# Sums over heads by moving the squares, products in two column halves, inverses from 16-row blocks

## The chip, the cores and the metric

One core of a Trainium2 chip runs the whole program. Its engines are PE (TensorE, matrix products; its weight loads have a row of their own, PEld), DVE (VectorE), ACT (ScalarE), POOL (GpSimd) and SP, which here only issues DMAs. The metric is the device time of one execution in microseconds (us); of three runs of the kernel before, the median was 831.88 us (831.33 to 832.63).

## The reference

Two decoder layers in float32 on 512 tokens of width 1024. Layer 0 mixes tokens with an RWKV-7 recurrence over 16 heads of 64 channels; layer 1 is a causal differential attention over shared keys and values. Each layer ends with a gated embedding ("ple"): `p[i] @ ple_w[i]`, gated by `sigmoid(h @ ple_gate[i])`. What the change touches:

```python
kk = k * k_k.reshape(H, N)
kk = kk / jnp.maximum(jnp.linalg.norm(kk, axis=-1, keepdims=True), 1e-12)
...
def step(state, inp):
    r_t, w_t, k_t, v_t, kk_t, a_t = inp
    s_kk = jnp.einsum('bhij,bhj->bhi', state, kk_t)
    state = (state * w_t[:, :, None, :]
             - s_kk[..., None] * (kk_t * a_t)[:, :, None, :]
             + v_t[..., None] * k_t[:, :, None, :])
    return state, jnp.einsum('bhij,bhj->bhi', state, r_t)
...
y = y + jnp.sum(r * k * r_k, axis=-1, keepdims=True) * v
...
e = p[i] @ ple_w[i]
g = jax.nn.sigmoid(h @ ple_gate[i])
h = h + rms_norm(g * e, ple_norm[i])
```

There are two sums over the 64 channels of a head for every token: the squared norm of `kk`, and the bonus `r * k * r_k`.

## The kernel before

**Dense products.** Every dense product is split in three fp32r products (`mm3`, L280 to L282: high by high, high by low, low by high), each 128x128 weights against 512 columns. There are 800 such triples. For each weight half-matrix of 512 columns (a "half") 32 triples run: 8 channel tiles by 4 blocks. The order of the halves in layer 0 is the table ORDER (L36): r, k and v of the first half of the channels, then of the second, then the two halves of the gate g. The ple products (16 triples a layer) come behind them (ple(0), L1331) and, for layer 1, behind its last projection.

**Recurrence.** The 16 heads are 8 channel tiles of two heads; tiles 0 to 3 are group 0 and 4 to 7 group 1. The 512 tokens are 8 chunks of 64. For each group: `decay(i)` (L668) makes the decays of a tile; `k_evac(i)` (L742) makes the scaled keys and both sums over heads; `gram` (L846) makes the 128x128 products of keys and queries of one pair of chunks, masked on DVE (L873); `inverse(n)` (L886, four batches) inverts the 64x64 unit triangular matrices of 16 heads-and-chunks; `operands` (L997) transposes and loads; `recur` (L1028) walks over the chunks; `finish` (L1132) normalises and gates.

**Sums over heads before.** `k_evac` holds the squares as weights (128x128 of `sq`) and moves the selector `hsel`, 2 columns wide: four products per tile (L756) for the norm, four (L789) with `rksel` for the bonus. An fp32 product is two records in the trace, so 32 instructions of a line are x64 there.

**Inverse before.** The 32x32 diagonal blocks are inverted by forward substitution on DVE, 31 steps of one multiplication (L927) and one addition (L930); the 64x64 inverse is put together from two sets of 32x32 products (L959, L973).

**A chunk of the recurrence before.** The state times keys and queries (L1059, 4 products of 128 columns), the masked products with the values (L1069, 8 of 64x64), a copy to SBUF (L1082), the inverse (L1085, 8), a copy (L1090), the state's update (L1098, 8) with two additions and two scalings on DVE (L1118, L1121), the outputs (L1104, 8), a copy (L1124). The 8 products of L1069, L1085 and L1104 all write one half of the 128 output partitions, `U` or `Y`; the 8 of L1098 write the two halves in turn, since its output rows are those of head 0 and head 1.

**What sets the order.** All instructions are placed by a planner in the file (class Streams, L65): every stage is a generator that yields an engine, an assumed duration and an instruction; a stage has a priority; the planner keeps a clock for every engine and issues what can start first. The order on PE, DVE, ACT and POOL is thus written out once and is fixed; each engine executes its instructions in that order and waits on semaphores. Where a step may go to one of two engines, the planner's clocks choose (PREF is how much sooner the later listed engine must be done). Names in the trace: `R` are 4 KB ring tiles, `H` 2 KB tiles, `p` the 8 PSUM banks (four shared by dense outputs, "pd", four by everything else, "pw"), `RAW` freshly loaded weights.

## Time and profile before

| | before |
|---|---|
| median of 3 runs | 831.88 us |
| profiled execution | 834.73 us, of which the span from first to last instruction is 832.9 us |
| mean granted PE clock | 0.977 |
| PE busy | 797.9 us (96%) |
| DVE busy | 617.2 us (74%) |
| ACT busy | 455.7 us (55%) |
| POOL busy | 175.0 us (21%) |
| DMA | 116.71 MB, mean 140 GB/s |

Rows of groups read: line, engine, operation, out<-in, shape, count, then busy time, mean ns of one, idle time of the engine just before them and what ended it. Matmuls overlap in the pipeline, so the mean ns of one is longer than the distance between two starts; prices are taken from starts in the timeline, whose rows are: start in us, duration in us, engine, line, operation, count of merged records. In the table of windows each engine's busy time (and records) in a stretch stands in the order PE, PEld, DVE, ACT, POOL, then the granted PE clock, the DMA share and GB/s.

### The profile page before, as it was taken

To read this page: it belongs to the slowest core of one execution; us is meant where nothing else is said; L and a number is where in the kernel's file an instruction comes from. 1 tells how busy PE (TensorE), PEld (TensorE's weight loads), DVE (VectorE), ACT (ScalarE), POOL (GpSimd) and SP (SyncE) were. 2 spreads that over 40 slices of the span, in tenths; PEclk is the share of its full clock that TensorE was granted. 3 is DMA by queue.
4 is the path that set the end of the run, shared out by engine and by line. 5 is a ranking of instruction groups with operands and counts; after the bars stand their busy time and mean duration, and the time that the engine had idled before them with its cause. 6 is when DMAs were issued, how large, how long until landed. Compare 5 with 4: busy or idle time off the path is not lost.

```text
span 832.9 us, 14128 instructions
## 1 busy us (share of the span) xinstructions
PE 797.9 (96%) x5224; PEld 657.5 (79%) x5224; DVE 617.2 (74%) x1463; ACT 455.7 (55%) x1041; POOL 175.0 (21%) x189
## 2 busy tenths in 40 slices
PE   6889999999998889999999999999999999999996
PEld 3677878878886668778888888888888888888885
DVE  3999689988649999998476786388864597934845
ACT  3788344658535464566334475387753586733431
POOL 3523214322303126844010011002000112000000
PEclk9998699999999799999999999999999999999999
DMA  7677357822314569235433353211203320334302
GB/s 302 222 265 258 114 197 264 309 92 90 127 31 150 199 218 320 73 128 177 158 129 127 127 175 103 101 52 52 89 14 102 101 92 11 128 101 152 128 25 101
DMA packets 40421, 116.71 MB, mean 140 GB/s; under 512 B 5152, under 2 KB 9632, under 8 KB 40352
## 3 DMA queue, kind: packets, MB, share of 16 engines
q1 hardware_dynamic: 35744, 99.03, 35.4%
q10 hardware_dynamic: 4608, 16.78, 5.1%
q8 instruction: 41, 0.67, 0.3%
q14 instruction: 28, 0.23, 0.1%
HBM read 90.63 MB, written 25.17 MB: 139 GB/s over the span
## 4 chain that ended last, share of the span: by engine, by line
PE 55%; DVE 2%; DMA 1%; issue 0%; ACT 0%; SPq 0%; DVEq 0%; POOLq 0%
PE p L280 15%; PE p L282 15%; PE p L281 15%; PE p L1624 2%; PE p L1589 1%; PE p L1291 1%; PE p L1588 1%; PE p L1615 1%; PE p L1460 1%; DMA R<-gD 1%; PE p L1663 0%; DVE R L1184 0%; DVE H L624 0%; DVE R L1167 0%; DVE R L1192 0%; PE p L1178 0%
## 5 line engine op out<-in xcount | busy, mean ns | idle before, releaser
L280 PE MATMUL p<-R,R 128*128 128x512 f32 x800 | 327.9, 410 | 0.9 <-DVE R L762 0.9
L281 PE MATMUL p<-R,R 128*128 128x512 f32 x800 | 315.3, 394 | 11.9 <-DVE R L489 11.8
L282 PE MATMUL p<-R,R 128*128 128x512 f32 x800 | 314.9, 394 | 0.0
L281 PEld LDWEIGHTS p<-R,R 128*128 128x128 f32 x800 | 152.1, 190 | 40.6 <-DVE R L489 14.3
L282 PEld LDWEIGHTS p<-R,R 128*128 128x128 f32 x800 | 151.6, 190 | 33.0
L280 PEld LDWEIGHTS p<-R,R 128*128 128x128 f32 x800 | 151.8, 190 | 32.3 <-DVE R L762 1.6
L313 DVE TENSOR_TENSOR R<-RAW,R 128x512 fp32r<-128x512 f32 x102 | 69.2, 689 | 32.1 <-ACT R L265 31.1
L313 POOL TENSOR_TENSOR R<-RAW,R 128x512 fp32r<-128x512 f32 x38 | 51.3, 1356 | 157.8 <-ACT R L265 59.7
L319 DVE SCALAR_TENSOR_TENSOR R<-RAW,vec,R 128x512 fp32r<-128x512 f32 x64 | 46.1, 748 | 34.3 <-ACT R L317 34.0
L265 ACT CAST R<-RAW 128x512 fp32r<-128x512 f32 x96 | 57.8, 617 | 9.2 <-DMA RAW<-in_w_k 6.2
L1278 POOL TENSOR_TENSOR hr<-hm,half 128x1 f32<-128x1 f32 x16 | 11.2, 702 | 167.5 <-DVE hm L1276 167.5
L317 ACT ACTIVATE R<-RAW,vec 128x512 fp32r<-128x512 f32 x64 | 44.1, 719 | 2.1 <-DMA RAW<-in_b_w_in 2.1
L276 POOL TENSOR_TENSOR orr<-orm,half 128x4 f32<-128x4 f32 x8 | 9.6, 1202 | 142.8 <-DVE orm L274 137.9
L1600 ACT ACTIVATE H<-p,mx 128x128 f32<-128x128 f32 (+3 forms) x64 | 33.4, 526 | 9.2 <-DVE mx L1597 8.4
L1311 ACT COPY R<-p 128x512 f32<-128x512 f32 x16 | 9.4, 589 | 48.8 <-PE p L282 48.6
L930 DVE TENSOR_TENSOR p<-p,H 128x126 f32<-128x126 f32 (+22 forms) x124 | 32.6, 263 | 4.3
L481 ACT ACTIVATE p<-R,omm 128x512 f32<-128x512 f32 x32 | 21.8, 689 | 20.1 <-DVE H L927 7.0
L1593 DVE CUSTOM_DVE_ANT_0 p<-p,cmask 128x128 f32<-128x128 f32 (+3 forms) x64 | 30.3, 508 | 2.6 <-PE p L1589 2.5
L927 DVE TENSOR_TENSOR H<-p,R 128x126 f32<-128x126 f32 (+22 forms) x124 | 30.9, 249 | 1.4
L1379 DVE SCALAR_TENSOR_TENSOR R<-H,R 128x512 f32<-128x512 f32 x16 | 11.1, 693 | 25.0 <-ACT H L1372 25.0
L873 DVE TENSOR_TENSOR R<-p,cmk 128x512 f32<-128x512 f32 x32 | 21.3, 683 | 10.4 <-PE p L864 10.3
L1372 ACT ACTIVATE H<-p 128x512 f32<-128x512 f32 x16 | 9.6, 597 | 34.1 <-PE p L282 34.1
(217 smaller groups left out, 1401.7 us busy)
## 6 DMA issues: line engine op xcount, KB each, us to landing
mD<-R ACTq DMA_DIRECT2D x32, 512.0 KB, 4.1
R<-mD SPq DMA_DIRECT2D x32, 512.0 KB, 5.3
RAW<-in_ple_gate SPq DMA_DIRECT2D x16, 512.0 KB, 3.5
RAW<-in_kv_w SPq DMA_DIRECT2D x16, 512.0 KB, 3.7
RAW<-in_b_w_in SPq DMA_DIRECT2D x16, 512.0 KB, 3.7
R<-in_x SPq DMA_DIRECT2D x8, 512.0 KB, 6.5
RAW<-in_w_r SPq DMA_DIRECT2D x8, 512.0 KB, 4.1
RAW<-in_w_k SPq DMA_DIRECT2D x8, 512.0 KB, 4.7
```

The lines of the kernel that those rows point to most:

```text
L265: (nc.scalar.copy if sc.eng == "ACT" else ENG[sc.eng].tensor_copy)(dst, src)
L280: nc.tensor.matmul(ps, ah, bh, start=first, stop=False)
L281: nc.tensor.matmul(ps, ah, bl, start=False, stop=False)
L282: nc.tensor.matmul(ps, al, bh, start=False, stop=last)
L313: ENG[sc.eng].tensor_sub(lo, f, hi.bitcast(F32))
L317: nc.scalar.activation(hi, f, AF.Copy, scale=g)
L319: nc.vector.scalar_tensor_tensor(lo, f, g, hi.bitcast(F32), ALU.mult, ALU.subtract)
L481: nc.scalar.activation(m, x_at(d), AF.Copy, scale=omm[:, c, d : d + 1])
L927: ve.tensor_mul(tmp[:, 0:m, 0:w], bc(xs[:, s_ : s_ + 1, 0:w], [P, m, w]), bc(nb[:, s_ + 1 : 32, s_ : s_ + 1], [P, m, w]))
L930: ve.tensor_add(xs[:, s_ + 1 : 32, 0:w], xs[:, s_ + 1 : 32, 0:w], tmp[:, 0:m, 0:w])
L1593: nc.vector.tensor_tensor_reduce(scs[m][:, 0:n], scs[m][:, 0:n], cmask[:, S - n : S], 1.0, -3.0e38, ALU.add, ALU.max, mx[:, m : m + 1])
L1600: nc.scalar.activation(E[m][:, 0:n], scs[m][:, 0:n], AF.Exp, bias=mx[:, m : m + 1], scale=0.125, accum_out=sm[:, m : m + 1])
```

## The change

1. **Sums over heads** (`head_sums`, `key_norms`, `bonus`). Now the selector is the weight (128 rows, 32 columns, two of them not zero) and the squares of a channel tile move, 512 columns. The four tiles of a group go to four column groups of 32, so one PSUM bank holds the sums of the group; it is copied to SBUF and transposed by four products, and the inverse norms of the whole group come from two DVE instructions on 128x32. A tile's keys can be scaled by the norm only when all four tiles have been squared. `r_k` is now multiplied in by ACT (`rkvec`, L842).
2. **Recurrence.** For odd channel tiles the two 64-row places (keys against removal keys, and so values against corrections) are swapped (PLACES, `crossed`), so that the 8 products of each set write the two halves of the output partitions in turn (`products`, L1134 to L1141, one line for what were L1069, L1085 and L1104). The products with the values now come before the product with the state, and everything accumulates in one bank; the inverse is held without its unit diagonal (`xm`). Each PSUM copy becomes two copies of half the columns, which ACT or DVE may take.
3. **Inverse.** The substitution on DVE is for 16x16 blocks, 15 steps; two sets of 64 products of 32x32 weights by 16 columns (L1016, on the four diagonal 32x32 tiles of the array) put the 32x32 inverses together; the step from 32 to 64 stays.
4. **ple.** Both layers' embedding products move into layer 0's table ORDER, before the first and behind the second half of g; their results go to DRAM (`peD`, 16 stores of 256 KB) and are loaded again at the end of each layer (8 loads).
5. **Planner.** PREF 0.0 to 0.15, FINP (priority of `finish`) from 4.5 and 6 to 7.5 and 7.6, and new assumed durations, so that the whole order changes.

On PE, around the first sums over heads (`H` are the squares, `ident` marks transposes, L280 to L282 the dense products). Before:

```order
L756 MATMUL p_823<-hsel_91,H_785 128x2 x4
L789 MATMUL p_833<-rksel_92,H_737 128x2 x4
L781 MATMUL p_831<-ident_86,H_813 128x128 x4
L781 MATMUL p_859<-ident_86,H_839 128x128 x4
L280 MATMUL p_857<-R_568,R_667 128x512
L281 MATMUL p_857<-R_568,R_667 128x512
L282 MATMUL p_857<-R_568,R_667 128x512
L789 MATMUL p_865<-rksel_92,H_745 128x2 x4
L789 MATMUL p_872<-rksel_92,H_753 128x2 x4
L781 MATMUL p_889<-ident_86,H_883 128x128 x4
```

With the change:

```order
L769 MATMUL p_761<-H_730,hsel_92 32x512
L769 MATMUL p_761<-H_739,hsel_92 32x512
L769 MATMUL p_761<-H_748,hsel_92 32x512
L769 MATMUL p_761<-H_756,hsel_92 32x512
L280 MATMUL p_785<-R_628,R_666 128x512
L281 MATMUL p_785<-R_628,R_666 128x512
L282 MATMUL p_785<-R_628,R_666 128x512
L780 MATMUL p_781<-ident_87,H_773 128x128 x4
L280 MATMUL p_801<-R_628,R_666 128x512
L281 MATMUL p_801<-R_628,R_666 128x512
L282 MATMUL p_801<-R_628,R_666 128x512
L831 MATMUL p_815<-ident_87,H_812 128x128 x4
```

The 2-column products scattered among the dense ones are gone; four 512-column products stand in their place, one dense triple ahead of their four transposes.

On DVE, around the sums of the second half of v (L598, now L603), while one batch of inverses is substituted (L927 and L930, now L984 and L987) and the first differences of g's input are made (L489, now L494). Before:

```order
L600 TENSOR_SCALAR vmean_89<-vmean_89 128x8 x2
L927 TENSOR_TENSOR H_2570<-p_2572,R_2680 128x16x8
L930 TENSOR_TENSOR p_2572<-p_2572,H_2570 128x16x8
L602 TENSOR_TENSOR H_2797<-H_2797,vmean_89 128x512
L927 TENSOR_TENSOR H_2570<-p_2572,R_2680 128x15x9
L930 TENSOR_TENSOR p_2572<-p_2572,H_2570 128x15x9
L602 TENSOR_TENSOR H_2805<-H_2805,vmean_89 128x512
L927 TENSOR_TENSOR H_2570<-p_2572,R_2680 128x14x9
L930 TENSOR_TENSOR p_2572<-p_2572,H_2570 128x14x9
L600 TENSOR_SCALAR vmean_89<-vmean_89 128x8
L489 TENSOR_TENSOR R_2700<-p_2701,R_2700 128x512
```

With the change:

```order
L605 TENSOR_SCALAR vmean_90<-vmean_90 128x8 x2
L984 TENSOR_TENSOR H_2832<-p_2846,H_2830 128x3x13
L987 TENSOR_TENSOR p_2846<-p_2846,H_2832 128x3x13
L607 TENSOR_TENSOR H_3017<-H_3017,vmean_90 128x512
L984 TENSOR_TENSOR H_2832<-p_2846,H_2830 128x2x14
L987 TENSOR_TENSOR p_2846<-p_2846,H_2832 128x2x14
L607 TENSOR_TENSOR H_3025<-H_3025,vmean_90 128x512
L984 TENSOR_TENSOR H_2832<-p_2846,H_2830 128x15
L987 TENSOR_TENSOR p_2846<-p_2846,H_2832 128x15
L605 TENSOR_SCALAR vmean_90<-vmean_90 128x8
L494 TENSOR_TENSOR R_2958<-p_2963,R_2958 128x512
```

Before, g's first difference stands behind all four v blocks with 14 of 31 substitution steps still to come; with the change it has been issued already (this L494 is the second), and the substitution ends at the same place.

On SP, PE's next work behind v is in these loads. Before, w_g follows w_v; with the change:

```order
L296 DMA RAW_2529<-in_w_v 128x1024
L296 DMA RAW_2608<-in_pT 128x1024
L480 DMA R_2577<-mD 128x1024
L480 DMA R_2643<-mD 128x1024
L296 DMA RAW_2680<-in_ple_w 128x1024
L480 DMA R_2702<-mD 128x1024
L480 DMA R_2754<-mD 128x1024
L480 DMA R_2794<-mD 128x1024
L296 DMA RAW_2805<-in_ple_w 128x1024
```

The 16 triples of ple(0) now lie between v and g on PE. The diff, cut:

```diff
-ORDER = [("r", 0), ("k", 0), ("v", 0), ("r", 1), ("k", 1), ("v", 1), ("g", 0), ("g", 1)]
+ORDER = [("r", 0), ("k", 0), ("v", 0), ("r", 1), ("k", 1), ("v", 1), ("p", 0), ("g", 0), ("g", 1), ("p", 1)]
-PREF = 0.0
+PREF = 0.15
-GRP, OPP, RECP, FINP = (5, 2.5), (4, 4), (0.3, 0.3), (4.5, 6)
+GRP, OPP, RECP, FINP = (5, 2.5), (4, 4), (0.3, 0.3), (7.5, 7.6)
...
+    PLACES = (slice(0, 4, 3), slice(1, 3))
     def parts(i):
-        return BK[i][:, :, 0:4:3, :], BK[i][:, :, 1:3, :], AR[i][:, :, 1:3, :]
+        x, y = PLACES[i % 2], PLACES[1 - i % 2]
+        return BK[i][:, :, x, :], BK[i][:, :, y, :], AR[i][:, :, y, :]
...
+    def head_sums(g, what):
+        for i in range(4 * g, 4 * g + 4):
+            yield "wait", (what, i)
+        yield "take", "pw", 1
+        pn = bank("pw")
+        yield "PE", 0.95, 0.25
+        for q in range(4):
+            nc.tensor.matmul(pn[32 * q : 32 * q + 32], hsel, SQ[what, 4 * g + q], start=True, stop=True)
+        yield "free", "H", 4
+        yield "take", "H", 1
+        t = HT([P, S])
+        yield "ACT", 0.52
+        nc.scalar.copy(t, pn)
...
+        for tb in range(NB):
+            nc.tensor.transpose(pt[:, tb * P : (tb + 1) * P], t[:, tb * P : (tb + 1) * P], ident)
...
     def k_evac(i, pk):
...
-        yield "PE!", 0.9, 0.02
-        for tb in range(NB):
-            nc.tensor.matmul(pn[:, 2 * tb : 2 * tb + 2], sq[:, tb * P : (tb + 1) * P], hsel, start=True, stop=True)
...
+        yield "wait", ("kn", g)
...
-        for tb in range(NB):
-            nc.tensor.matmul(pb[:, 2 * tb : 2 * tb + 2], sq[:, tb * P : (tb + 1) * P], rksel[:, i, :], start=True, stop=True)
...
     def inverse(n):
...
-        for s_ in range(31):
-            m, w = 31 - s_, s_ // 2 + 1
...
+        for s_ in range(15):
+            m, w = 15 - s_, s_ + 1
...
+        for lhs, rhs in ((None, xT), (x32, w32)):
+            yield "take", "pw", 1
+            ps = bank("pw")[:, 0 : 16 * 16].rearrange("p (a j) -> p a j", j=16)
+            yield "PE", 1.3, 0.5
+            for hd in range(16):
+                for q, r in enumerate(quads):
+                    block = lower(q, hd // 8, hd // 4 % 2)[:, hd % 4 // 2, hd % 2, 32 * (q % 2) : 32 * (q % 2) + 32]
+                    nc.tensor.matmul(ps[r, hd], lhs[r, hd] if lhs is not None else block, rhs[r, hd, 0:16], start=True, stop=True)
...
     def recur(g):
...
+            def products(out, x, off, rhs, start):
+                for n, (ii, hh) in enumerate(crossed):
+                    o = off[ii % 2 ^ par]
+                    nc.tensor.matmul(
+                        out[HALF[par][ii % 2 ^ x], cols(ii, hh)], G[cq, hh, g][:, ii, par, o : o + HN], rhs[:, cols(ii, hh)],
+                        start=start and n < 2, stop=True, skip_group_check=True,
+                    )
...
+            products(pA, 0, AOFF, uv, True)
             if c_ > 0:
-                yield "PE", 1.05
+                yield "wait", ("state", c_, g)
+                yield "PE", 1.0
...
+            for x in range(2):
+                yield "ACT/DVE!" if x == 0 else "ACT/DVE", (0.3, 0.35)
+                copy(tiles_of(gt, x)[HALF[par][x]], tiles_of(pA, x)[HALF[par][x]])
+            yield "PE", 0.55
+            products(pA, 0, AOFF, gt, False)
...
     def pe_evac(l, hf, tb, ps):
...
+        nc.sync.dma_start(peD[l, tb, :, hf * S : (hf + 1) * S], t)
...
+    def pe_load(l):
...
+            nc.sync.dma_start(pe[l, tb], peD[l, tb])
```

More of the change, by code (lines that the diff above doesn't have):

```diff
@@ new lines, in key_norms, with bonus @@
+    def key_norms(g):
+        pt = yield from head_sums(g, "sq")
+        c2 = CK[g] = T(ax, [P, NB, 4, 2], "c2", bufs=2)
+        yield "DVE", 0.15
+        nc.vector.tensor_scalar(c2, pt, 1e-24, None, ALU.max)
+        yield "DVE", 0.25
+        nc.vector.reciprocal(c2, c2)
+        yield "free", "pw", 1
+        yield "set", ("kn", g)
+    def bonus(g):
+        pt = yield from head_sums(g, "rk")
+        yield "ACT", 0.2
+        nc.scalar.copy(bon[:, :, 4 * g : 4 * g + 4, :], pt)
+        yield "free", "pw", 1
+        yield "set", ("bonus", g)
@@ L931, in inverse @@
-        yield "free", "H", 1
-        yield "free", "R", 1
-        yield "take", "R", 1
-        xr = R([P, 32, 2, 16])
-        yield "DVE", 1.14
-        nc.vector.transpose(xr, bc(xs.unsqueeze(3), [P, 32, 16, 2]))
-        yield ("free", "pw", 1) if eng == "DVE" else ("free", "H", 1)
+                    copy(four(na[r, 8 * u + 4 * hh : 8 * u + 4 * hh + 4]), lower(q, u, hh)[:, :, :, 32 * (q % 2) : 32 * (q % 2) + 32])
+        yield "take", "H", 1
+        nb = HT([P, 16, 32])
+        yield "DVE", 1.05
@@ L946, in inverse @@
-        yield "DVE+", 1.06
-        nc.vector.scalar_tensor_tensor(xv, xr[:, :, 1, :], rowm[:, 1:2], xv, ALU.mult, ALU.add)
-        yield "free", "R", 1
+        xv = x32.rearrange("p h (d r) -> p r d h", d=2)
+        for d in range(2):
+            yield "ACT/DVE+!" if d == 0 else "ACT/DVE+", (0.45, 0.35)
+            if sc.eng == "ACT":
+                nc.scalar.activation(xv[:, :, d], xr[:, :, d], AF.Copy, scale=rowm[:, d : d + 1])
+            else:
+                nc.vector.tensor_scalar(xv[:, :, d], xr[:, :, d], rowm[:, d : d + 1], None, ALU.mult)
@@ L999, in operands @@
         gsl = slice(g * 512, g * 512 + 512)
+        for i in range(4 * g, 4 * g + 4):
+            yield "wait", ("rk", i)
         for c_ in range(NC):
@@ L1355, in pe_evac @@
     def pe_evac(l, hf, tb, ps):
+        yield "take", "H", 1
+        t = HT([P, S])
         yield "ACT", 0.48
-        nc.scalar.copy(pe[l, tb][:, hf * S : (hf + 1) * S], ps)
-        yield "free", "pw", 1
-        yield "set", ("pe", l, hf, tb)
+        nc.scalar.copy(t, ps)
+        yield "free", "pd", 1
+        yield "DMA", 0.7
+        nc.sync.dma_start(peD[l, tb, :, hf * S : (hf + 1) * S], t)
+        yield "free", "H", 1
+        yield "set", ("kept", l, hf, tb)
+    def pe_load(l):
+        for tb in range(NB):
+            for hf in range(2):
+                yield "wait", ("kept", l, hf, tb)
+            yield "take", "R", 1
+            pe[l, tb] = R([P, D])
+            yield "DMA", 1.4
+            nc.sync.dma_start(pe[l, tb], peD[l, tb])
+            yield "set", ("pe", l, tb)
     hn = {}
@@ L1681, in trunk @@
         yield "wait", ("filled",)
-        yield from ple(0)
         yield from layer_end(0, half_act(zF), z_ready, I["x"], 8)
```

280 lines of the change are left out of this document (137 added, 143 removed).

## The prediction, made before the change was timed

> **What bounds the kernel now.** I read the page first, for the engine that is never free, then the table of windows for the stretches where it is not full or not at full clock, then PE's waits, then the timeline of the products that the change touches.
>
> ```profile
> PE 797.9 (96%) x5224; PEld 657.5 (79%) x5224; DVE 617.2 (74%) x1463; ACT 455.7 (55%) x1041; POOL 175.0 (21%) x189
> PE 55%; DVE 2%; DMA 1%; issue 0%; ACT 0%; SPq 0%; DVEq 0%; POOLq 0%
> 735.18 0.40 PE L280 MATMUL p<-R,R 128*128 128x512 f32 x1
> 735.87 0.39 PE L280 MATMUL p<-R,R 128*128 128x512 f32 x1
> 180.00:200.00 20.00, 19.78 (x299) 16.24 (x298) 14.36 (x28) 15.74 (x44) 2.85 (x6) 1.00 0.36 120
> ```
>
> PE is busy 96% of the span and is the chain. A dense triple costs 0.69 us from start to start, so the 800 triples are some 550 us that the change leaves alone. A gain has to come from the other PE work, from the 35 us in which PE is idle, or from stretches of half clock. The last row is a recurrence stretch: 299 small records among few triples, PE full, clock 1.00.
>
> ```profile
> 85.00:90.00 5.00, 4.28 (x28) 3.68 (x27) 4.93 (x12) 2.34 (x6) 3.71 (x3) 0.87 0.40 113
> 90.00:95.00 5.00, 5.00 (x23) 4.71 (x21) 3.48 (x7) 1.87 (x4) 0.08 (x1) 0.50 0.40 149
> 95.00:100.00 5.00, 5.00 (x21) 4.67 (x21) 1.41 (x2) 0.51 (x3) 0.00 (x0) 0.50 0.27 108
> 100.00:105.00 5.00, 5.00 (x24) 3.68 (x23) 2.51 (x5) 1.00 (x2) 0.00 (x0) 0.50 0.26 105
> 272.00:275.00 3.00, 1.54 (x6) 0.89 (x8) 2.90 (x10) 0.02 (x1) 1.50 (x2) 0.50 0.97 335
> 275.00:278.00 3.00, 3.00 (x19) 2.45 (x18) 2.73 (x10) 0.67 (x1) 0.00 (x0) 0.50 0.92 369
> PE p L281 <- DVE R L489: 11.8, 5, 6.7
> 273.46 0.79 PE L281 MATMUL p<-R,R 128*128 128x512 f32 x1 [6.75 <-DVE R L489]
> 293.17 0.50 PE L281 MATMUL p<-R,R 128*128 128x512 f32 x1 [1.50 <-DVE R L489]
> 302.74 0.50 PE L281 MATMUL p<-R,R 128*128 128x512 f32 x1 [1.11 <-DVE R L489]
> ```
>
> Two places are not at their best. From about 88 to 105 us PE is full but at clock 0.50: this is where the first group's sums over heads run, products of 2 columns. DVE, nearly full until 90, empties, so PE sets the pace: at 0.87 and three times 0.50 about 8 us are lost. From 266 to 303 PE waits for DVE, which is full with the substitution and v's means and only then makes g's input differences: 6.75 + 1.50 + 1.11 = 9.4 us idle, and about 3 us more at half clock behind the long one.
>
> **The products in two halves.**
>
> ```profile
> L1085 PE MATMUL p<-H,R 128*64 128x64 f32 x256 | 18.3, 225 | 0.6 <-ACT H L1082 0.5 <-POOL H L1080 0.2
> 353.38 1.07 PE p L1085 x16
> 360.06 1.07 PE p L1069 x16
> 355.97 0.69 PE L1098 MATMUL p<-R,R 128*64 128x64 f32 x16
> 356.49 1.10 PE L1104 MATMUL p<-R,R 128*64 128x64 f32 x16
> ```
>
> Eight instructions (16 records) that write one half cost 1.07 us. The eight of L1098, of the same shape, write the halves in turn, and the next group starts 0.52 us behind them. The trace thus shows the very form that L1069, L1085 and L1104 get. 16 chunks by 3 groups are 48, times 0.55: **-26.4 us**. PE is full there, so this is path time. Bounds: the chain's own 0.62 for L1098 (not quoted; start to start is the direct price) would leave 0.45 a group, -21.6; none if accumulating into one bank keeps the halves from overlapping, a rival below.
>
> **The sums over heads.**
>
> ```profile
> 87.34 0.99 PE L756 MATMUL p<-hsel,H 128*128 128x2 f32 x8
> 88.19 1.40 PE L789 MATMUL p<-rksel,H 128*128 128x2 f32 x8
> 10.51 1.02 PE L529 MATMUL p<-R,R 128*128 128x512 f32 x2
> 12.22 1.02 PE L529 MATMUL p<-R,R 128*128 128x512 f32 x2
> 361.73 0.44 PE p L1178 x4
> ```
>
> Eight records of 2 columns take 0.85 us (87.34 to 88.19) at full clock. L756 and L789 have 64 records each: 13.6 us go. New are four head sums of four 512-column fp32 products. L529 and L530 in turn give the serial price: four records from 10.51 to 12.22, 0.43 each, so 3.44 us a head sum if nothing overlaps. If all four column groups ran side by side it is one instruction's two records, 0.86. I take 2.1: records keep their order, the second record of a product must wait for its first on the same columns, so at any time two groups run, five slots of 0.43. That is my reading of the pair in L1098 (a gain of two, not more), not something shown for four groups. So +8.5 (3.4 to 13.8), and 16 transposes at 0.11, +1.8. Net **-3.3 us** (-8.4 to +2.0).
>
> The Trainium skill (TensorE: Matmul & The Clock Gate, on the measured speedup of packing) gives 2.38 times for three column tiles of 32 at 512 columns; by that ratio four would take about 1.1 us (an estimate), and the sum would be 4 us lower. It speaks of single products, not of fp32's pairs of records, and no row here shows it.
>
> **The half clock at 88 to 105.** 512 moving columns keep PE at work as a dense triple does, so the clock should hold. But DVE sets the pace until 90 (4.93 of 5), a tile's keys now wait for the norms of all four, and PE, rid of its small products, will wait instead for k's banks. I count **-5 us** of the 8 (0 to -8).
>
> **The inverses.**
>
> ```profile
> 161.62 1.20 PE L973 MATMUL p<-H,H 32*32 32x32 f32 x64
> L973 PE MATMUL p<-H,H 32*32 32x32 f32 x256 | 5.0, 192 | 0.0
> L927 DVE TENSOR_TENSOR H<-p,R 128x126 f32<-128x126 f32 (+22 forms) x124 | 30.9, 249 | 1.4
> L930 DVE TENSOR_TENSOR p<-p,H 128x126 f32<-128x126 f32 (+22 forms) x124 | 32.6, 263 | 4.3
> ```
>
> PE gets 512 products (L1016), 1024 records, of 32x32 weights by 16 columns. The nearest row has the same weights and 32 columns: 64 records in 1.20 us, 0.018 each. At that price 18.4 us; if only columns count, half, 9.2. A line through 0.032 (64 columns, L1098) and 0.018 (32) gives 0.011 for 16, 11.3 us. I take **+13 us**, nearer the line.
>
> The Trainium skill (TensorEngine Tiling, Instruction Overhead) says that each matmul carries about 60 cycles, so that narrow ones gain nothing; 25 ns a record (an estimate from its 60 cycles) would make L1016 25.6 us and the whole 12 us worse. The trace is below that already at 32 columns (18 ns), so the measurement decides.
>
> On DVE, 248 instructions of 63.5 us become 120 of about 0.24, 29 us; transposes and selections about even out, and 18 copies come in. DVE falls by some 35 us.
>
> **The waits on DVE at 266 to 303.** Substitution is shorter, g's first difference now stands ahead of v's means, and 16 triples of ple(0), 16 x 0.69 = 11 us that need no difference, lie between v and g. They cover the 6.75 us. I count **-10 us** of the 12.4 (0 to -12.4). ple itself costs the same elsewhere; its 24 DMAs add 8.4 MB to 116.71 MB on queues that PE never waits for but at the start; peD is loaded while the 64 triples of the output product run. It leaves the end of the attention, where it was cover:
>
> ```profile
> 733.59 1.05 PE L1624 MATMUL p<-R,H 128*128 128x128 f32 x8
> 737.02 1.13 DVE L1657 SCALAR_TENSOR_TENSOR H<-p,orr,R 128x128 f32<-128x128 f32 x4
> ```
>
> The last unit's chain runs from PE's end at 734.6 to DVE's end at 738.15, 3.6 us; the new order leaves six triples there, 4.1 us. So nothing; without that cover it would be 3.6 us.
>
> **New waits in the recurrence.**
>
> ```profile
> L1082 ACT COPY H<-p 64x512 f32<-64x512 f32 x16 | 9.3, 579 | 13.8 <-PE p L1069 13.7
> L1022 ACT COPY R<-p 128x128 f32<-128x128 f32 x64 | 12.3, 278 | 10.5 <-PE p L1019 10.3
> PE p L1059 <- DVE R L1121: 0.8, 2, 0.7
> PE p L1085 <- ACT H L1082: 0.5, 1, 0.5
> ```
>
> Each copy of 0.58 becomes two of about 0.38 (between 0.28 at 128 columns and 0.58 at 512), 0.2 more when one engine takes both. Behind a waiting product on PE stand dense triples, for which everything waits. Before, such waits were 1.3 us in all; the order now often leaves one triple (0.69) or less between state product and second product. I add **+2.5 us** (0 to +10: 32 hand-offs by 0.3).
>
> **Sum.** -26.4 - 3.3 - 5 + 13 - 10 + 2.5 = -29.2 us. It is made against the profiled execution's span of 832.9 us (its own time was 834.73, 1.8 more around the span): 803.7. Applied to the median of the runs, 831.88, it gives **803 us**.
>
> **The rivals.** *Better than that:* four column groups side by side (3.4), L1016 at half price (9.2), both DVE stretches cured: -26.4 - 8.4 - 8 + 9.2 - 12.4 + 1 = -45, 787 us. For it speaks that DVE loses 35 us; against it that 80 to 90 stays DVE's. *Fixed prices:* a small product costs the same whatever its width (L1016 at 0.018, +5.4) and the head sums run one after another (+5.3): 814 us. The equal shapes of L973 and L1098 at different prices speak against the first; nothing yet against the second. *No overlap of the products:* with accumulation in one bank the 26.4 us stay, about 829 to 832. L1098 alternates within one bank too, which speaks against it. *Slower:* the chain of a chunk becomes the bound in `recur`. PE's part of a chunk falls by 1.65 us while the chain (state product, copies, inverse, copies, update on DVE) gets longer, and the order is fixed, so uncovered hand-offs stop everything behind them. It decides from 29/16 = 1.8 us of waiting per chunk, 0.9 us at each of the two copies; at 1.2 us a copy it costs 38 us and the kernel takes about 841. Against it: copies waited 0.5 us in total so far.
>
> **How the numbers follow.** Forecast (795 to 810) 55%; better 20%; fixed prices (810 to 822) 15%; no overlap 4%; slower 6%. The range is 787 to 819: it leaves out the last two cases and the far ends of two others, 2 in 10. This kernel's runs differ by 0.16%, so 0.2% is about what can be told from no change: faster 0.90, within 0.2% 0.03, slower 0.07.
>
> **What would show it.** Right: L1138's groups of 16 records about 0.52 us apart, L1016's 128 records in about 1.6 us, L769's 8 in about 2.1; clock 1.00 soon behind the first head sum; no wait of 6 us at g's first triple; DVE near 580 us busy, PE near 775. Wrong: 1.07 for L1138; PE waits at L1138 from ACT or DVE of more than 10 us in all; clock 0.5 in a recurrence stretch; a wait for peD.

## The result and the profile after

The changed kernel takes 827.26 us (median of 6 runs, 825.34 to 830.43), the kernel before 832.34 us on the same chip (6 runs, 831.33 to 833.52): a ratio of 0.9934 with a 95% interval of 0.9911 to 0.9957. It is faster, by some 5 us, where 29 were forecast, and lies outside the range of 787 to 819. The profiled execution took 827.46 us against 834.73, so 7.3 us less, and that is the difference taken apart here.

The page of the changed kernel, with PE's and its weight loads' row, the chain, and of the DMA queues the one that brings instructions (packets, MB, share):

```profile
span 825.7 us, 16116 instructions
PE 780.7 (95%) x6168; PEld 628.9 (76%) x6168; DVE 587.6 (71%) x1342; ACT 473.8 (57%) x1105; POOL 175.0 (21%) x208
PE 76%; DVE 13%; ACT 6%; issue 3%; DMA 1%; DVEq 0%; POOL 0%; ACTq 0%; SPq 0%; POOLq 0%
q8 instruction: 48, 0.79, 0.4%
```

The same queue of the kernel before:

```profile
q8 instruction: 41, 0.67, 0.3%
```

DVE's 588 us and PE's 781 are near the forecast's 580 and 775. New is "issue" with 3% of the chain, where the kernel before showed 0%: PE stood still and waited for nothing that the profile shows. The groups of the new products, by shape (busy us and mean ns of one record; records overlap, so the price of a group is read from start to start), and PE's waits (total, times, longest):

```profile
L1138 PE MATMUL p<-R,R 128*64 128x64 f32 x512 | 21.9, 228 | 1.8 <-issue 1.8
L1138 PE MATMUL p<-H,R 128*64 128x64 f32 x256 | 11.0, 228 | 2.7 <-DVE H L265 1.9 <-ACT H L265 0.8
L1016 PE MATMUL p<-H,H 32*32 32x16 f32 x512 | 7.0, 193 | 6.6 <-issue 6.6
L1016 PE MATMUL p<-H,R 32*32 32x16 f32 x512 | 5.3, 180 | 0.5 <-DVE H L1006 0.5
L769 PE MATMUL p<-H,hsel 128*32 128x512 f32 x32 | 4.8, 605 | 0.0
```

```profile
PE p L1016 <- issue: 6.6, 4, 2.9
PE p L281 <- DVE R L494: 3.6, 4, 1.3
PE p L920 <- issue: 2.1, 1, 2.1
PE p L1138 <- DVE H L265: 1.9, 1, 1.9
PE p L1138 <- issue: 1.8, 1, 1.8
PE p L1037 <- issue: 1.3, 1, 1.3
```

The wait of 6.75 us at g's first triple is gone, as forecast. In its place stand pauses of 1.3 to 2.9 us in front of L1016, L920 and L1037. (The one at L1138 is something else: it ends at 295.80, and L1065's last copies into that operand end at 295.70, so I take it for a wait that the profile did not name.)

```profile
293.56 2.14 ACT L1065 COPY R<-p 32x128 f32<-32x128 f32 x8
295.72 0.58 ACT L492 CAST R<-p 128x512 fp32r<-128x512 f32 x1
```

```profile
295.80 0.78 PE L1138 MATMUL p<-R,R 128*64 128x64 f32 x16 [1.77 <-issue]
```

And the half clock has moved. In the windows (last three columns: granted clock, DMA share, GB/s) 80 to 100 us is nearly cured, but two stretches of the recurrences are now at 0.80 and 0.83. The first of these was at 0.74 before, behind the wait of 6.75 us; the second was at full clock. Before:

```profile
80.00:100.00 20.00, 19.09 (x100) 17.17 (x99) 14.79 (x30) 8.19 (x19) 7.53 (x6) 0.72 0.40 143
260.00:280.00 20.00, 13.25 (x58) 10.29 (x57) 19.14 (x63) 8.72 (x22) 5.63 (x6) 0.74 0.47 172
300.00:320.00 20.00, 18.89 (x180) 14.99 (x179) 18.24 (x58) 11.94 (x30) 5.27 (x7) 1.00 0.82 286
```

With the change:

```profile
80.00:100.00 20.00, 18.04 (x109) 12.39 (x108) 18.98 (x36) 15.22 (x29) 9.97 (x8) 0.91 0.62 203
260.00:280.00 20.00, 15.04 (x322) 11.98 (x321) 10.73 (x22) 8.71 (x16) 4.38 (x6) 0.80 0.90 317
300.00:320.00 20.00, 17.19 (x412) 14.29 (x410) 11.70 (x27) 8.58 (x24) 7.58 (x11) 0.83 0.83 284
```

**Where the time went.** The 800 dense triples come in the same number in both kernels, so the starts of the 97th and the 321st cut each trace into three stretches with equal dense work. The table is worked out from the two traces. "Pauses" are idle time of PE with no releaser that begins at a 256th instruction (below), "waits" all other idle time; "half clock" is half of the time that PE was busy at a granted clock of 0.5; "work" is the rest. All in us:

```
                             length   work   pauses   waits   half clock
to the 97th       before      106.5   88.6     0       6.7      11.2
                  after        96.2   86.5     0       8.0       1.7
97th to 321st     before      295.5  278.9     0      13.4       3.2
                  after       294.3  264.8    10.3     9.2      10.0
321st to the end  before      398.9  398.9     0       0         0
                  after       401.7  399.6     0       2.1       0
```

(After loses another 1.6 us before the first triple and behind the last.) In the middle stretch, with all inverses and recurrences, 14.1 us of PE's work did go and waits fell by 4.2; pauses and half clock took 17.1 back.

### The profile page after: what moved, and what is told of

Same layout as the page of the kernel before. It is cut to its first block, busy times and chain, and to the rows that moved or that the text cites. A ratio compares the mean times of both kernels' runs of the same rounds, so it can differ in the third digit from the quotient of the medians.

```text
span 825.7 us, 16116 instructions
## 1 busy us (share of the span) xinstructions
PE 780.7 (95%) x6168; PEld 628.9 (76%) x6168; DVE 587.6 (71%) x1342; ACT 473.8 (57%) x1105; POOL 175.0 (21%) x208
## 4 chain that ended last, share of the span: by engine, by line
PE 76%; DVE 13%; ACT 6%; issue 3%; DMA 1%; DVEq 0%; POOL 0%; ACTq 0%; SPq 0%; POOLq 0%
PE p L280 19%; PE p L282 18%; PE p L281 18%; PE p L1138 3%; PE p L920 2%; PE p L1706 2%; PE p L1151 1%; PE p L1016 1%; PE p L1360 1%; ACT R L265 1%; PE p L1671 1%; PE p L1670 1%; PE p L1697 1%; PE p L1179 1%; DVE R L265 1%
## 5 line engine op out<-in xcount | busy, mean ns | idle before, releaser
L280 PE MATMUL p<-R,R 128*128 128x512 f32 x800 | 329.2, 411 | 1.9 <-ACT R L492 1.4
L282 PE MATMUL p<-R,R 128*128 128x512 f32 x800 | 314.8, 394 | 0.0
L280 PEld LDWEIGHTS p<-R,R 128*128 128x128 f32 x800 | 151.6, 189 | 36.2 <-ACT R L492 2.8
L282 PEld LDWEIGHTS p<-R,R 128*128 128x128 f32 x800 | 151.3, 189 | 33.0
L313 POOL TENSOR_TENSOR R<-RAW,R 128x512 fp32r<-128x512 f32 x42 | 56.5, 1352 | 155.2 <-ACT R L265 95.8
L313 DVE TENSOR_TENSOR R<-RAW,R 128x512 fp32r<-128x512 f32 x98 | 67.5, 703 | 9.5 <-ACT R L265 8.8
L265 ACT CAST R<-RAW 128x512 fp32r<-128x512 f32 x103 | 62.4, 620 | 10.0 <-DMA RAW<-in_ple_gate 3.4
L1460 DVE SCALAR_TENSOR_TENSOR R<-H,R 128x512 f32<-128x512 f32 x16 | 11.1, 691 | 23.9 <-ACT H L1453 23.9
L488 DVE SCALAR_TENSOR_TENSOR p<-R,vec,p 128x511 f32<-128x511 f32 x32 | 23.7, 749 | 6.0 <-ACT p L486 5.9
L1670 PE MATMUL p<-R,R 128*128 128x256 f32 (+1 forms) x96 | 25.0, 291 | 0.0
L265 ACT CAST R<-R 64x512 fp32r<-64x512 f32 (+1 forms) x29 | 17.9, 619 | 11.7 <-DVE R L1260 11.2
```

The lines of the kernel that those rows point to most:

```text
L265: (nc.scalar.copy if sc.eng == "ACT" else ENG[sc.eng].tensor_copy)(dst, src)
L280: nc.tensor.matmul(ps, ah, bh, start=first, stop=False)
L282: nc.tensor.matmul(ps, al, bh, start=False, stop=last)
L313: ENG[sc.eng].tensor_sub(lo, f, hi.bitcast(F32))
L488: nc.vector.scalar_tensor_tensor(m[:, 1:], x_at(d)[:, 0 : S - 1], vcol(V_MU + c, d), m[:, 1:], ALU.mult, ALU.add)
L1670: nc.tensor.matmul(s_[:, sl], qh[:, m, x, :], kt, start=True, stop=False)
```

## Experiments

**The theory.** Each place where PE pauses has one thing in common. If PE's weight loads, products and the semaphore instructions between them are counted together in order of their start (12,458 in all), the pauses of the recurrences, seven of 0.3 to 2.9 us, begin at 1473, 1729, 2497, 2753, 5057, 5313 and 6337: each time 193 behind a multiple of 256. The page of the profile says what comes in portions of this size: 48 packets of 0.79 MB are 16 KB each, and 12,458 is 48.7 times 256. Before, 41 packets came for 10,561, 41.3 times 256. So PE's instructions come in blocks of 256, and my theory was that a block of tiny products is used up before the next one is there ("supply"). One burst of L1016, 64 products, is 128 records and 128 loads: exactly one block in 1.2 to 1.4 us at full clock. The timeline around the longest pair of pauses:

```profile
270.17 0.60 PE L920 MATMUL p<-R,R 64*128 64x128 f32 x5
272.87 0.80 PE L920 MATMUL p<-R,R 64*128 64x128 f32 x3 [2.11 <-issue]
273.60 1.89 PE L1016 MATMUL p<-H,H 32*32 32x16 f32 x124
278.34 0.29 PE L1016 MATMUL p<-H,H 32*32 32x16 f32 x4 [2.85 <-issue]
```

From the first to the second pause lie 3 + 124 products, which with 128 loads and one semaphore instruction are 256; the pauses don't respect the program's groups but cut L920 behind 5 records and L1016 behind 124. In the kernel before, the fastest block took 5.4 us, and there was no such pause. The rivals: hand-offs of the recurrence that the profile fails to name ("chain"), and big transfers that hold the DMA engines when a block is due (0.90 and 0.83 busy in the windows of the longest; "contention").

**The supply by itself.** To the end of the kernel before, where nothing else is left to do:

```diff
     sc.run()
+    for width, count in ((16, 512), (32, 256), (64, 128)):
+        ps = bank("pw")
+        rows = 64 if width == 64 else 32
+        for n in range(count):
+            ...
+            nc.tensor.matmul(ps[r, c : c + width], ident[r, 0:rows], ident[r, 0:width], start=True, stop=True)
```

> The kernel before with extra products at its end, whose results nothing reads: 512 of 32x16 (four 32-row, 32-column corners of the array in turn), then 256 of 32x32, then 128 of 64x64, when the data queues carry next to nothing. Supply theory: in the first burst (8 blocks of 256 instructions at 2.4 to 2.9 us) a pause at every 256th instruction, 1 to 3 us each, so that a block takes 3.4 to 5.5 us; in the second (5.1 us a block) pauses under 0.5 us; in the third (9.5 us a block) none. Theory of contention (the blocks are late only where big transfers hold the DMA engines, 0.80 to 0.95 busy at the pauses): no pauses over 0.4 us in any of the three. Chain theory: no pauses either. Time: before's plus 35 to 60 us.

884.55 us (one run), and the timeline at its end:

```profile
828.83 1.81 PE L1721 MATMUL p<-ident 32*32 32x16 f32 x194
833.19 1.90 PE L1721 MATMUL p<-ident 32*32 32x16 f32 x128 [2.55 <-issue]
837.47 1.90 PE L1721 MATMUL p<-ident 32*32 32x16 f32 x128 [2.38 <-issue]
841.20 1.90 PE L1721 MATMUL p<-ident 32*32 32x16 f32 x128 [1.82 <-issue]
...
859.29 1.93 PE L1721 MATMUL p<-ident 32*32 32x32 f32 x128 [2.07 <-issue]
863.29 1.93 PE L1721 MATMUL p<-ident 32*32 32x32 f32 x128 [2.07 <-issue]
870.75 11.03 PE L1721 MATMUL p<-ident 32*32 32x32 f32 x318 [1.52 <-issue]
```

Every 128 records PE stops for 1.5 to 2.6 us, in step with nothing but the count. Ten blocks, from 833.19 to 870.75, take 37.6 us: 3.76 us a block, 15 ns an instruction, though the records themselves need 1.9 us at the half clock that came with the pauses. The DMA engines were 0.07 busy from 829 to 871, so contention falls as the cause of the pauses. Whether big transfers make a pause longer stays open: in the changed kernel, of two blocks that PE waited for, one came 3.46 us behind the block before it with the DMA engines 0.02 busy (160.73 to 164.19), the other 5.47 us with 0.93 (272.87 to 278.34). I had the 32-column products' own time too long (1.93 a block, not 5.1), so they pause as well. The 64-column products fill 4.5 us a block and don't pause. The Trainium skill (Runtime: NRT & Kernel Launch, Instruction fetch mechanics) states the block of 16 KiB, 256 instructions, with which the count agrees; it also says that the fetch is hidden because dispatch is slower than the refill, and there the traces differ: at 7.5 ns of own time an instruction it is not hidden, at 17.6 it is.

**The same program, counted from elsewhere.** In front of everything, where PE waits 6 us for its first input:

```diff
+    seed = T(cp, [P, 32], "seed")
+    nc.gpsimd.memset(seed, 0.0)
+    first = bank("pw")
+    for n in range(32):      # 16 in the second kernel
+        nc.tensor.matmul(first[0:32, 0:16], seed[0:32], seed[0:32, 0:16], start=True, stop=True)
```

> The changed kernel with 32 tiny products (128 instructions) in front of all matrix-engine work, where it waits 6 us for its first input anyway; every other instruction and its order stay. Supply theory: pauses still begin where the count from the start of the kernel is 193 modulo 256, so at places of the program 128 instructions earlier than in the changed kernel, in other groups; number and length 6 to 14 us in all, time 820 to 832. Chain theory (hand-offs cause the pauses): they stay at the same products, whose count is now 65 modulo 256, with 827.

> The same with 16 products (64 instructions). Supply theory: pauses at 193 modulo 256 again, 64 instructions earlier in the program than in the changed kernel, time 820 to 832. Chain theory: at 1 modulo 256 (193 and 64), 827.

827.95 us (825.32 to 829.71; 0.9925, 0.9893 to 0.9958) and 830.52 us (826.84 to 834.68; 0.9962, 0.9925 to 1.0). The same burst of L1016 that the changed kernel cuts behind 124 of its 128 records is now cut elsewhere. With 32 products ahead:

```profile
270.30 0.69 PE L1022 MATMUL p<-H,H 32*32 32x16 f32 x60
273.80 1.15 PE L1022 MATMUL p<-H,H 32*32 32x16 f32 x68 [2.81 <-issue]
```

With 16:

```profile
274.55 1.00 PE L1022 MATMUL p<-H,H 32*32 32x16 f32 x92
278.76 0.72 PE L1022 MATMUL p<-H,H 32*32 32x16 f32 x36 [3.21 <-issue]
```

(L1022 is L1016 there.) 64 and 32 records earlier, just the 128 and 64 instructions put in. All six and seven pauses of the recurrences over 0.4 us start at 193 modulo 256 of the new count. The unnamed wait at L1138, 1.3 us in both kernels, is not among them: it stays in front of the same products, as a hand-off does. No hand-off of the program moves as the pauses do: the chain theory of the pauses falls. They sum to 10.0 and 14.2 us, against 10.3.

In these three kernels every pause of 1.3 us or more went with a stretch of 3.4 to 10.2 us at clock 0.50 that began during it or within 1.6 us of its end (in the changed kernel 20.5 of the 23.9 us of half clock in the middle stretch); none under 1 us brought on a new one. That the pause causes it is what this order suggests; nothing was tried on the clock alone.

**Is PE's work what counts there at all?** The order of a group's eight products turned, so that four in a row go to one column half:

```diff
-                for n, (ii, hh) in enumerate(crossed):
+                for n, (ii, hh) in enumerate(sorted(crossed, key=lambda y: y[0] % 2)):
...
-                        start=start and n < 2, stop=True, skip_group_check=True,
+                        start=start and n % 4 == 0, stop=True, skip_group_check=True,
```

> The changed kernel with the order of the eight products inside each group turned (L1138): the four of one column half first, then the four of the other, everything else in the same order. Term 1 of the prediction (the halves run side by side only where consecutive products go to different halves): a group of 16 records takes 1.05 us, not 0.61, 21 us more matrix-engine work. If that work sets the end of the recurrences: time 845 to 850. Supply theory: the same, less 2 to 4 us, since a slower group gives the next block of instructions time (pauses 10.3 to 6 or 8 us). If the chain of hand-offs or the vector engine sets it: under 835. If the halves never mattered: 0.61 stays and 827.

837.15 us (833.5 to 838.41; 1.0042, 1.002 to 1.0064):

```profile
L1138 PE MATMUL p<-R,R 128*64 128x64 f32 x512 | 30.5, 228 | 1.8 <-issue 1.8
L1138 PE MATMUL p<-H,R 128*64 128x64 f32 x256 | 15.4, 228 | 1.6 <-DVE H L265 1.3 <-ACT H L265 0.3
```

Start to start, a group takes 0.88 us, not 0.61 and not the expected 1.05, so 13 us more work; the kernel takes 9.9 more. Halves that alternate do matter, and PE's work sets most of the recurrences' length. Pauses stayed (11.0 us): the slower groups did not give the blocks time where L1016 needs it.

**Taking the pauses away.** First by leaving room for a dense triple between pieces of a burst (Gap is a stage of no engine):

```diff
-            yield "PE", 1.3, 0.5
             for hd in range(16):
+                if hd % 4 == 0:
+                    if hd > 0:
+                        yield "Gap", 0.7
+                    yield "PE", 0.33, 0.5
```

> After's own instructions and results, in another order: each of the two bursts of 64 products in an inverse (L1016) is cut into four pieces of 16, and the planner keeps 0.7 us between two pieces, room for one dense triple. Supply theory (the matrix engine's instructions come in blocks of 256, and a block that is used up in less than about 5 us leaves the engine without instructions; in the changed kernel all seven pauses of 0.3 to 2.9 us marked 'issue', 10.3 us in all, begin at every 256th instruction): pauses fall to 2 to 5 us, the half clock that follows them goes with them in part, time 812 to 821 us. Chain theory (the pauses belong to hand-offs of the recurrence, the place in the instruction count is chance): the inverse's chain is 4.2 us longer in each of four batches, pauses stay at 9 to 12 us, time 827 to 835.

And pieces of 8 (`hd % 2`), with L1037 and L1051 in two pieces:

> As e1_spread, but pieces of 8 products, and the two products of the 64-blocks (L1037, L1051 of the changed kernel) cut into two pieces as well. By instruction counts and the changed kernel's times per record only one block of 256 instructions would still take under 5 us (5.0), against eleven before. Supply theory: pauses marked 'issue' under 1.5 us, no half-clock stretch of 7 us or more between 260 and 330, time 805 to 814. Chain theory: the inverse's chain is 11 us longer in each batch, which the recurrence then waits for: time 830 to 845, pauses as before.

827.66 us (822.24 to 829.25; 0.99, 0.9852 to 0.9947) and 832.16 us (830.97 to 833.8; 0.9974, 0.9952 to 0.9995). The pauses are gone, 0.8 and 0.2 us left; the time is not. (The traced execution of the first took 822.24 us, the lowest of its four; the others took 827.54 to 829.25. So its row shows some 5 us of gain that the median doesn't have.) In the middle stretch:

```
                       length   work   pauses   waits   half clock
after                   294.3  264.8    10.3     9.2      10.0
pieces of 16            290.1  269.3     0.8    16.0       4.0
pieces of 8             302.3  278.0     0.2    15.4       8.7
```

Two things ate the gain. Each cut costs work: 24 cuts 4.5 us, 64 cuts 13.2, some 0.2 us for each time that PE turns from tiny to dense products and back. And waits for DVE come up, in pieces of 16 above all the state product L1154 for the state's update L1197 and the products for their copies:

```profile
PE p L1154 <- DVE R L1197: 6.2, 5, 2.6
PE p L1141 <- ACT H L265: 2.5, 2, 1.3
PE p L1182 <- DVE R L745: 1.9, 1, 1.9
```

My reading is that the pauses had partly stood in for such waits: while PE stood, DVE caught up.

Are these waits only planned too tight? The planner's reckoning from a vector or scalar step's end to its user, in pieces of 16 and in the kernel with 32-block inverses that follows:

```diff
-    LATENCY = {"DMA": 2.4, "PE": 0.2, "ACT": 0.14, "DVE": 0.13, "Pool": 0.09}
+    LATENCY = {"DMA": 2.4, "PE": 0.2, "ACT": 0.5, "DVE": 0.5, "Pool": 0.09}
```

> e1_spread with one more edit: the planner reckons 0.5 us, not 0.13 and 0.14, from the end of a vector or scalar step to its user, so that it puts more dense work between the steps of a chunk. In e1_spread the matrix engine waited 10.4 us for such steps in the first recurrence and its second (L1154 for the state update 6.2, the products and S = K.U for copies 4.2), with a half-clock stretch of 6.8 us behind. Theory that these hand-offs, planned too tight, are what is left once the supply pauses are gone: waits for L1197 and L265 fall under 4 us, time 812 to 820. Theory that the vector engine's own work or the order of keys sets the recurrence's end: the waits move to other places, time 822 to 832.

> e3_inv32 (32-block inverses, 821.2 us) with the same planner edit as e5_spread_slack. Hand-off theory: waits of the matrix engine between 160 and 330 fall from 20 us to under 10, time 808 to 816. Theory of the vector engine (with 32-block inverses it is busy 0.83 of 120 to 340 us): no gain, 819 to 828.

840.12 us (1.0089, 1.0059 to 1.0118) and 843.86 us (1.0145, 1.0094 to 1.0196). In the first, waits in the middle stretch are 16.1 us where they were 16.0, at other places, and its length is 290.1 us as before; the loss lies in the second layer, 414.8 us against 401.6. Slack everywhere is a bad remedy, and the waits are not a matter of a few tenths of reckoning.

**The parts of the change that set the pauses.** The inverse as before (31 steps on DVE, no L1016):

```diff
-        na, eye, tmp = HT([P, 16, 32]), HT([P, 16, 16]), HT([P, 15, 16])
+        na, xs, tmp = HT([P, 16, 32]), HT([P, 32, 16]), HT([P, 31, 16])
...
-        for s_ in range(15):
+        for s_ in range(31):
...
-        for lhs, rhs in ((None, xT), (x32, w32)):
-            ...
```

> The change without its third part: 32-block inverses on the vector engine as before (31 steps), no L1016. Supply theory: no pauses marked 'issue' over 0.3 us; 12 us of matrix-engine work, 10.3 us of pauses and up to 10 us of half clock go, the wait for the vector engine at the second inverse (6.8 us before) and its half clock (5 us) come back: 808 to 816 us. Chain theory: 12 us of work goes, 12 us of waits come back: 825 to 830.

The stages of ple back behind the first layer's dense work, still through memory:

```diff
-ORDER = [..., ("v", 1), ("p", 0), ("g", 0), ("g", 1), ("p", 1)]
+ORDER = [..., ("v", 1), ("g", 0), ("g", 1)]
...
         yield "wait", ("filled",)
+        yield from ple(0)
...
         yield "spawn", gain("post1", ("dense", "b", 3)), 5
+        yield "spawn", ple(1), 8
```

> The change without its sixth part: the two stages of 16 triples (ple) stand where they stood before, after all dense work of the first layer, and go through the same buffer in memory. Prediction's term 6 (the move itself is worth nothing, its 16 triples cover the wait for the vector engine): time 827 to 837, a wait of some us at the second group's start. Theory that the moved stages take banks and transfers from the recurrence: 815 to 823.

And both:

> Both undone, the 16-block inverse (e3_inv32, 821.2) and the moved stages (e7_ple_back, 819.8): what is left of the change are the head sums, the products in two halves and the new copies. If the two losses are separate: 6 and 7 us off 827.3, 812 to 817. If both take away the same half clock and waits of the second group's start: 817 to 822.

The medians, with the ratio to the kernel before:

```
                     ple moved                             ple at its old place
16-block inverse     827.26  0.9934 (0.9911 to 0.9957)     819.77  0.9846 (0.9813 to 0.9879)
32-block inverse     821.20  0.9828 (0.9786 to 0.9870)     829.06  0.9940 (0.9921 to 0.9960)
```

Either part undone makes the changed kernel faster, both undone make it no faster: the two don't add. The middle stretch shows why (the traced executions took 827.46, 819.21, 824.20 and 827.58 us, so the third lies 3 us over its median):

```
                           length   work   pauses   waits   half clock
16-block, moved             294.3  264.8    10.3     9.2      10.0
16-block, old place         287.0  264.7     5.2    11.2       5.8
32-block, moved             291.2  253.9     0      23.7      13.6
32-block, old place         296.0  254.3     0      26.2      15.5
```

Without L1016 there is no pause and 10 to 11 us less work, but 14 to 15 us more waits for DVE, with half clock behind them. With both undone, PE waits for g's input differences as it did in the kernel before:

```profile
PE p L281 <- DVE R L494: 7.8, 7, 2.4
PE p L280 <- ACT R L492: 7.2, 4, 3.0
PE p L1136 <- DVE R L1179: 4.3, 3, 2.4
```

The 16 triples of ple cover some of that, so with 32-block inverses their move is worth 7.9 us. With 16-block inverses there is little left to cover. Their old place lets other dense work fall between the second group's bursts; the two pauses of 2.11 and 2.85 us are not there, and half clock falls by 4.2 us. The DMA engines are 0.43 busy there from 260 to 280 us, not 0.90, so the transfers may have a part in it; no run separates the two:

```profile
PE p L1016 <- issue: 3.5, 3, 1.6
PE p L1051 <- issue: 0.9, 1, 0.9
```

**Together.** ple at its old place and bursts cut three times as in pieces of 16, or once, with room for three triples:

> Pieces of 16 products in the inverse (e1_spread) and the stages of ple at their old place (e7_ple_back). Supply theory: no pauses over 0.5 us (5.2 in e7_ple_back), 4 us of matrix-engine time for the additional switches between tiny and dense products as in e1_spread, half clock at most one stretch of 6.8: 812 to 820. If pauses only hide waits for the vector engine, as in e1_spread's first recurrence (16.0 us of other waits against 9.2): 818 to 826.

> e7_ple_back (819.8 us) with each burst of 64 products in an inverse cut once, into two pieces of 32, and 2.1 us between them, room for three dense triples: 8 additional switches between tiny and dense products where pieces of 16 had 24 (which cost 5 us of matrix-engine time in e1_spread and e12). Supply theory: pauses of e7_ple_back (5.2 us) under 2, work 266 to 267 us between the 97th and the 321st dense triple, 814 to 819. If the waits for the vector engine take the place of the pauses whatever the pieces are (11.2 to 15 us): 819 to 824.

821.76 us (0.9861, 0.9825 to 0.9898) and 822.01 us (0.9882, 0.9848 to 0.9916): neither is better than 819.77. Pauses are 0.7 us in both, where 5.2 were. The first pays 5.8 us of work and 3.7 of waits for it, the second 2.8 (0.35 us for each of its 8 cuts) and 2.1.

**The planner's numbers.** In the kernel with ple at its old place, the preference of 0.15 us and the finish's place set back (`PREF = 0.0`, `FINP = (4.5, 6)`), then the finish's place alone, then the preference alone and only from the second layer's attention on:

> e7_ple_back with the planner's other two numbers of the change undone (the preference of 0.15 us for the first engine named, and the later place of the finish of the chunks). The prediction gave these no term. If they are worth nothing: 818 to 822. If they keep vector work off the recurrences, as the remaining 11 us of waits would suggest: 824 to 832.

> e7_ple_back with only the place of the chunks' finish set back (4.5 and 6). In e14_ple_back_pref, where the preference was undone too, 24.3 us of waits stood between the 97th and the 321st dense triple (11.2 in e7), 16 of them at 358 to 385 before the finish's transposes and the second layer's first dense work. If the finish's place makes these: 835 to 845. If the preference does: 819 to 824.

> e7_ple_back (819.8 us) with the planner's preference of 0.15 us set back to 0 from the start of the second layer's attention on. In the changed kernel, and in every run with 0.15, the 479 dense triples from the 321st to the last take 401.6 us with 2.1 us of waits; in the kernel before and in e14_ple_back_pref, both with 0, 398.9 and none. If the preference does that: 2.7 us less, 816 to 818. If the later finish of the chunks does it: 819 to 821.

844.26 us (1.0129, 1.0091 to 1.0167), 836.02 us (1.0042, 1.0015 to 1.0069) and 818.37 us (817.64 to 819.67; 0.9821, 0.9789 to 0.9853). The finish's later place, which had no term in the forecast, is worth 16 us. Undoing the preference as well costs another 8 us (844.26 against 836.02): in the traces the middle stretch then takes 310.2 us, not 302.7, and the last stretch 398.9, not 401.7. So beside the finish's old place the preference helps in the first layer and costs in the second; I had expected 832 at most for both undone. With the finish's old place alone, DVE's second state update (L1194) stands behind the finish's L1260, which waits for a transfer, and the next chunk's state product on PE behind that. This wait is 4.9 of the 11 us by which the waits of the middle stretch rise:

```profile
359.31 0.42 DVE L1191 TENSOR_TENSOR R<-R,p 64x256 f32<-64x256 f32 x1
361.41 1.13 DVE L1260 SCALAR_TENSOR_TENSOR R<-p,vec,R 128x128 f32<-128x128 f32 x4 [1.67 <-DMA R<-gD]
362.56 0.42 DVE L1194 TENSOR_TENSOR R<-R,pcall 64x256 f32<-64x256 f32 x1
```

```profile
363.04 1.97 PE L1151 MATMUL p<-R,R 128*128 128x128 f32 x8 [4.86 <-DVE R L1194]
```

And the preference costs the second layer 2.7 us. The window 420 to 800 of the changed kernel, then of the last experiment, PE busy first:

```profile
420.00:800.00 380.00, 377.86 (x1967) 318.55 (x1966) 258.28 (x646) 215.44 (x508) 38.22 (x48) 1.00 0.32 106
```

```profile
420.00:800.00 380.00, 380.00 (x1972) 321.17 (x1971) 257.39 (x654) 211.76 (x500) 34.04 (x44) 1.00 0.33 111
```

The 479 triples from the 321st on take 398.9 us again, without a wait. This kernel is the fastest here, 1.8% ahead of the kernel before. Its lead over the one with ple back alone (819.77, intervals overlap) is shown for that stretch, not for the whole time.

## Why the prediction was wrong

The direction was right, and PE's work in the recurrences came close: -14.1 us, where terms 1, 4 and the second group's half of term 2 make -15. In part that is luck, since term 1 gave 5 us less than forecast and the other two some 3 us more. What failed is the step that priced L1016.

1. **Products in halves**, -26.4 forecast: 29.5 us instead of 51.1 for the three lines, -21.6, the bound that the prediction named. A group takes 0.61 us, not 0.52. The trace shows where the difference lies. The 16 starts of a group take 0.46 us in L1138 as in L1098, but what follows starts 0.15 us behind the last of them, not 0.05: L1098 was followed by L1104, of the same shape, and L1138's groups are followed by other shapes. The price was read at the one place that has no change of shape behind it.

```profile
207.50 0.69 PE L1138 MATMUL p<-R,R 128*64 128x64 f32 x16
208.12 1.16 PE L1151 MATMUL p<-R,R 128*128 128x128 f32 x8
```

2. **Head sums**, -3.3 forecast: the 32 records of L769 cost 4.5 us, 1.0 us for three of the head sums and 1.5 for the first, not 2.1 each; transposes 1.6. So 13.6 us became 6.1, -7.5. In three of the four sums the first records of the four products start within 20 ns and their second records 0.45 us later, so all four column groups run side by side, and my reading of records as five slots was wrong. The estimate of 1.1 us from the ratio in the Trainium skill (TensorE: Matmul & The Clock Gate, Measured speedup vs the span model) was for single products, and the trace, with 1.0, agrees with it for fp32's pairs.
3. **Half clock at 88 to 105**, -5 forecast: 8.5 us became 1.7, -6.8. A stretch of 3.4 us behind the wait for L826 (1.9 us) is what is left. (The table's 11.2 us before the 97th triple hold another 2.6 at 61 to 68 us, behind waits of 1.75 and 0.96 us at L675. They went too, and no term had them.) No run changed the head sums alone, so that they are what holds the clock up is not shown.
4. **L1016**, +13 forecast: its records cost 11.7 us, 0.009 to 0.011 each at full clock, close to what the line through two widths gave. **This is the step that failed.** It took the price of a record as the whole price of a burst. 64 products are 256 instructions, and a block of 256 that is used up in 1.4 us meets a supply of one block in some 3.8 us (e4). That cost 10.3 us of pauses and went with most of the 6.8 us of additional half clock, together up to 17 of the 22 us that are missing. How much of that the pauses really cost is not shown: they covered waits at the same time, and with the pauses taken away (pieces of 16) the middle stretch became 4 us shorter in the trace and the median of the runs no better. Instruction queue and record counts stood on the page of the kernel before, but no row of it showed a pause. The estimate of 25 ns a record from the Trainium skill (TensorEngine Tiling (Array Packing), Instruction Overhead), which I set aside because 18 ns stood in the trace, would have made L1016 25.6 us. Work and pauses together are 22, nearer to that than to 13, but for another reason: at full supply the trace has 9 to 11 ns.
5. **Waits for DVE**, -10 forecast: the 6.75 us at g are gone, and all waits of the middle stretch with the new ones of term 7 fell from 13.4 to 9.2, -4.2 against a forecast of -7.5. The 16-block inverse is what cures them (26.2 against 11.2 without and with it, ple at its old place), not the cover by ple.
6. **The move of ple**, 0 forecast: +7.5 us with this inverse, -7.9 with the old one. The prediction had it as cover for a wait that the shorter inverse cures by itself. This is the second step that failed.
7. **New waits in the recurrence**, +2.5 forecast: 2.7 us at L1138 for copies, 1.2 at L1179 and the unnamed 1.8 at L1138, 5.7 in all, inside its bounds. The slower rival (the chunk's chain) did not come. It is near, though: take away PE's pauses, and waits rise to 16 us.

Not in the sum at all: the planner's preference (+2.8 us in the second layer; in the first it helps, at least beside the finish's old place) and the finish's place (16 us, measured with ple at its old place).

Among its signs of being wrong the prediction named "clock 0.5 in a recurrence stretch". That sign came, but from a cause that none of the rivals held.

What stays open: why waits for DVE rise in the first recurrence when the pauses go. DVE is 17.5 of 20 us busy there (200 to 220 us, pieces of 16) and its order is fixed, so its own load is likely; no run took load off it alone.

## What to carry to other kernels

A tiny product has two prices: its time on the array and its share of the instruction supply. Count instructions (an fp32 product is four) in every burst: where 256 of them are used up in less than about 4 us, as the records' price has it, reckon with the supply's time and with half clock behind the pause, or mix the burst with big products and pay for the switches (here that took the pauses away, but gained nothing that the medians show). Where several parts of a change cure the same wait, price them against each other: here each of two parts gained 8 to 9 us without the other and lost 6 to 8 us beside it.

## What was not expected of the hardware

- PE's instructions come in blocks of 16 KB (48 packets, 0.79 MB), one in 3.76 us on the mean (3.45 to 4.28) with nearly idle DMA engines: 15 ns an instruction, about 30 ns for a record with its weight load. Inside a block the records of 32x16 run at 9 to 11 ns at full clock.
- A pause stands at the same count from the start of the kernel whatever the program does there: 64 instructions put in at the front move the cut from 124 to 92 records, 128 to 60.
- Four fp32 products of 512 columns in four column groups take 1.0 us together (three of four times; 1.5 the first), where one alone is two records of 0.43.
- A turn from a burst of tiny products to dense ones and back cost 0.2 us of PE (24 cuts 4.5 us, 64 cuts 13.2), in one kernel 0.35 (8 cuts 2.8). From the last record of L1138 to a product of another shape are 0.15 us; from L1098's to one of the same shape it was 0.05.
- The eight products of one group, four in a row to one half, take 0.88 us; in the kernel before, with all eight to one half, 1.07; alternating 0.61.
